# Starting the feed-forward part with the half-token products of two weight pairs, and making their weight sums later

## Chip, core and metric

The kernel runs on one core of one Trainium2 chip. The metric is the device time in microseconds (us), as the median of several executions. One execution was also taken with the hardware profiler; it stands beside the others below. Engines are named as the profile names them: PE (TensorE), PEld (its weight loads), DVE (VectorE), ACT (ScalarE), POOL (GpSimd) and SP (SyncE, which here only issues DMAs). "Lnnn" is a line of the kernel's source.

## The reference

Two layers of a transformer-like block run over 512 tokens of width 1024, all in float32. The change touches the second half of each layer: the norm, the input product of the feed-forward part and what follows.

```python
D_MODEL = 1024
SEQ = 512
DEPTH = 2
FFN_HIDDEN = 2816
...
        x = x + merged @ w_out[i]
        hn = rmsnorm(x, norm2_g[i])
        gate, up = jnp.split(hn @ w_ffn_in[i], 2, axis=-1)
        x = x + (jax.nn.silu(gate) * up) @ w_ffn_out[i]
```

Ahead of these lines stand a combined input projection, a pool mixer, a differential attention and a gated merge, which the change leaves as they are.

## The kernel before

**Precision.** Every float32 operand is cut into a high and a low part of type float32r, `hi` and `lo`, and a product is three matmuls: hi by hi, hi by lo, lo by hi (`product` L243, `pair_product` L253). The usual cut (`split` L177) is a cast on ACT (L179) and a subtraction on DVE (L180). A second form (`parts` L207 with a piece number) relieves DVE: ACT casts the high part (L214), copies it negated into the low part (L215), and POOL issues a DMA that adds the weights from memory on top of it (L216).

**Seven products instead of eight.** The feed-forward input works on pairs of hidden tiles. A pair has 256 gate columns and 256 up columns, and each of its four weight pieces is 512 rows by 256 columns (128x1024 in memory, 512 KB): A11 and A12 are the gate's first and second half of rows, A21 and A22 the up's. The activations are cut the same way into halves of rows and halves of tokens, B11 and B21 for tokens 0 to 255 and B12 and B22 for tokens 256 to 511. A scheme of the Strassen kind makes the four output blocks with seven products of 24 matmuls each (128x256). The class `Ffn` numbers them: 1 is A11 by B11, 2 is A12 by B21, 4 is A22 by T4, and 3, 5, 6, 7 multiply the weight sums S4, S1, S2, S3 (made on DVE, L672 to L678) with B22 and the activation sums T1, T2, T3. Products 1 and 2 need tokens 0 to 255 alone; all others need all 512 tokens. `first` runs product 1, `second` product 2, `rest` the other five in the order 6, 5, 7, 3, 4 (with product 2 between 5 and 7 where it was not done yet), and `swiglu` makes the hidden tile.

**Where the activations come from.** `project_out` (L605) adds the output projection to the residual `res` (L599) token tile by token tile (four tiles of 128). After each tile `normed` (L294) is issued: a square with a sum on ACT (L298), a small operation on DVE (L276), a power on POOL (L277), and two multiplications on DVE into `xs` (L302). `normed` puts the transposition of `xs` on PE (L267, eight 128x128 matmuls) into a list of later work, which is due when a given amount of matmul work has been issued, or when `need` (L285) asks for it. `Quarters.put` (L337) follows each transposition: for tiles 0 and 1 it makes B11 and B21, for tiles 2 and 3 it makes T1 to T4 and B22 out of the transposed values and those of tile 0 or 1 (tiles `xd`; parts `xqh`, `xql`, `xrh`, `xrl`, `xth`, `xtl`; L357 to L367).

**The order around the change.** After `project_out` the first pair (f0 = 0) loads its four pieces, makes all its sets and sums, runs products 1 and 2, waits by `need` for tiles 2 and 3, and runs `rest`. Then the second pair (f0 = 2) begins, with product 2 within `rest`, and so on for eleven pairs in three rounds, with the feed-forward output product after each round. `weight_plan` (L47) lists the pieces in the order in which SP loads them.

**Buffers.** Raw pieces and one sum per pair (`ws`) share seven buffers (`RAWS`), the cut sets six pairs of high and low buffers (`SPLITS`). PSUM has three `mm` tiles, two `sc` tiles (the accumulator `self.a` of products 1 and 2) and two `tr` tiles (the transpositions, and product 4). A scheduler places each engine's instructions when the program is built; at run time each engine takes its instructions strictly in that order.

## Time and profile before

| quantity | value |
|---|---|
| median of 3 runs | 1466.33 us (1463.86 to 1468.88) |
| the profiled execution's own time | 1463.79 us |
| its span, first to last instruction | 1461.9 us |
| mean granted TensorE clock | 0.995 |
| DVE busy | 978.4 us (67%) |
| ACT busy | 698.8 us (48%) |
| POOL busy | 120.6 us (8%) |
| DMA, mean over the span | 118 GB/s |

The span is what the profile's pages count from; the execution's own time is 1.9 us longer. Two stretches per execution concern the change, one for each layer: from the first matmul of product 1 (378.88 us in layer 0, 1102.80 us in layer 1) to the first matmul of the third pair (432.72 and 1156.51 us). Busy times in the profile count an instruction from its start to its modelled end, so that neighbours overlap; the distance from one start to the next is what a row of work costs.

### The profile page before, as it was taken

The page shows a single profiled execution, that of the slowest core. Times are in us where ns is not written, and L with a number is a line of the kernel's source. Part 1 is how long each engine was busy: PE and PEld are TensorE (multiplying, and loading weights), DVE is VectorE, ACT ScalarE, POOL GpSimd, SP SyncE. Part 2 cuts the span into 40 slices and gives each one's busy share as a digit, 9 for nine tenths or more (in the row PEclk, how much of TensorE's full clock was granted, in tenths as well). Part 3 has the DMA queues.
Part 4 walks back from the last instruction along what each step waited for, and adds up shares of the span by engine and source line. Part 5 has one row for each costly group of instructions (what it writes and reads, how often), then busy time and mean ns, then how long its engine had stood idle before and what let it go on. Part 6 is the DMA issues. An engine that isn't in the chain of part 4 may idle for free.

```text
span 1461.9 us, 21648 instructions
## 1 busy us (share of the span) xinstructions
PE 1437.6 (98%) x8390; PEld 1267.7 (87%) x8390; DVE 978.4 (67%) x1816; ACT 698.8 (48%) x1323; POOL 120.6 (8%) x153
## 2 busy tenths in 40 slices
PE   8999999999799999999999999999997999999999
PEld 6888888888699989989888888888887998999897
DVE  7767666666788548736576686666758885487472
ACT  6544353453666346516355443435446663464350
POOL 1010000000101001001010001000001110010000
PEclk9999999999999999999999999999999999999999
DMA  7321231223358447817422132222323774586261
GB/s 278 108 73 62 90 116 58 87 88 99 87 146 191 139 126 179 216 43 207 140 86 81 58 116 80 72 80 68 127 59 101 176 197 114 135 185 176 66 166 58
DMA packets 49784, 173.02 MB, mean 118 GB/s; under 512 B 5649, under 2 KB 6545, under 8 KB 49682
## 3 DMA queue, kind: packets, MB, share of 16 engines
q1 hardware_dynamic: 38882, 134.41, 28.0%
q0 software_dynamic: 9504, 34.61, 13.3%
q10 hardware_dynamic: 1296, 2.62, 0.6%
q8 instruction: 66, 1.08, 0.3%
q14 instruction: 36, 0.29, 0.1%
HBM read 169.52 MB, written 2.10 MB: 117 GB/s over the span
## 4 chain that ended last, share of the span: by engine, by line
PE 95%; DVE 3%; ACT 1%; issue 1%; POOL 0%; DMA 0%; POOLq 0%; DVEq 0%
PE mm L248 19%; PE mm L250 19%; PE mm L249 19%; PE mm L262 6%; PE mm L263 6%; PE mm L260 6%; PE sc L260 3%; PE sc L262 3%; PE sc L263 3%; PE tr L267 3%; PE tr L263 1%; PE tr L262 1%; PE tr L260 1%; DVE wlo L180 1%; PE sc L250 1%; DVE xs L302 1%
## 5 line engine op out<-in xcount | busy, mean ns | idle before, releaser
L179 ACT CAST whi<-raw 128x1024 fp32r<-128x1024 f32 x222 | 233.2, 1052 | 197.3 <-issue 118.7
L180 DVE TENSOR_TENSOR wlo<-raw,whi 128x1024 fp32r<-128x1024 f32 x222 | 270.0, 1220 | 83.9 <-ACT whi L179 79.1
L248 PE MATMUL mm<-whi,xh 128*128 128x512 f32 x512 | 206.1, 402 | 0.1
L250 PE MATMUL mm<-whi,xl 128*128 128x512 f32 x512 | 200.6, 392 | 0.0
L249 PE MATMUL mm<-wlo,xh 128*128 128x512 f32 x512 | 200.5, 392 | 0.1
L599 DVE TENSOR_TENSOR res<-mm,res 128x512 f32<-128x512 f32 (+1 forms) x97 | 66.0, 683 | 118.1 <-PE mm L250 118.0
L250 PE MATMUL mm<-whi,fl 128*128 128x512 f32 (+1 forms) x358 | 138.5, 387 | 0.0
L248 PE MATMUL mm<-whi,fh 128*128 128x512 f32 (+1 forms) x358 | 138.3, 387 | 0.0
L249 PE MATMUL mm<-wlo,fh 128*128 128x512 f32 (+1 forms) x358 | 138.2, 387 | 0.0
L277 POOL TENSOR_TENSOR r<-r,mhalf 128x1 f32<-128x1 f32 (+1 forms) x80 | 62.0, 774 | 671.8 <-DVE r L276 567.4
L250 PEld LDWEIGHTS mm<-whi,xl 128*128 128x128 f32 x512 | 96.3, 188 | 21.1 <-DVE xl L180 0.2
L248 PEld LDWEIGHTS mm<-whi,xh 128*128 128x128 f32 x512 | 96.6, 189 | 18.5 <-ACT xh L179 0.6
L249 PEld LDWEIGHTS mm<-wlo,xh 128*128 128x128 f32 x512 | 96.7, 189 | 17.9 <-DVE wlo L180 0.5
L216 POOL DMA_DIRECT2D wlo<-in_wts x66 | 57.9, 877 | 619.1 <-ACT wlo L215 322.3
L260 PE MATMUL sc<-xqh,whi 128*128 128x256 f32 x352 | 101.9, 289 | 0.7 <-ACT whi L214 0.7
L248 PE MATMUL mm<-xh,whi 128*128 128x512 f32 x256 | 102.0, 398 | 0.0
L260 PE MATMUL mm<-xrh,whi 128*128 128x256 f32 x352 | 99.8, 284 | 1.9 <-ACT xrh L179 1.9
L262 PE MATMUL sc<-xql,whi 128*128 128x256 f32 x352 | 101.1, 287 | 0.0
L263 PE MATMUL sc<-xqh,wlo 128*128 128x256 f32 x352 | 101.0, 287 | 0.0
L262 PE MATMUL mm<-xrl,whi 128*128 128x256 f32 x352 | 99.8, 284 | 0.9 <-DVE xrl L180 0.9
L260 PE MATMUL mm<-xqh,whi 128*128 128x256 f32 x352 | 99.8, 284 | 0.3
L250 PE MATMUL mm<-xh,wlo 128*128 128x512 f32 x256 | 99.9, 390 | 0.0
(161 smaller groups left out, 3463.5 us busy)
## 6 DMA issues: line engine op xcount, KB each, us to landing
raw<-in_wts SPq DMA_DIRECT2D x244, 512.0 KB, 4.3
wlo<-in_wts POOLq DMA_DIRECT2D x66, 512.0 KB, 7.5
pwr<-in_pool_w ACTq DMA_DIRECT2D x8, 256.0 KB, 2.6
out<-res SPq DMA_DIRECT2D x7, 256.0 KB, 2.0
res<-in_x SPq DMA_DIRECT2D x3, 512.0 KB, 8.2
g<-in_gains SPq DMA_DIRECT2D x6, 256.0 KB, 3.1
res<-in_x ACTq DMA_DIRECT2D x1, 512.0 KB, 3.7
lv<-in_rows SPq DMA_DIRECT2D x2, 256.0 KB, 5.7
```

Of the source, the lines that this page charges most:

```text
L179: ins = nc.scalar.copy(hi, src)
L180: nc.vector.tensor_sub(lo, src, hi.bitcast(F32))
L216: nc.gpsimd.dma_start(lo.rearrange("p a b -> p (a b)"), wts[piece_no], accum_op=ALU.add)
L248: nc.tensor.matmul(acc, lhsT=ah, rhs=bh, start=i == 0, stop=False)
L249: nc.tensor.matmul(acc, lhsT=ah, rhs=bl, start=False, stop=False)
L250: nc.tensor.matmul(acc, lhsT=al, rhs=bh, start=False, stop=i == n - 1)
L260: nc.tensor.matmul(acc[:, i, :], lhsT=ah, rhs=bh, start=start and not i and not k, stop=False, skip_group_check=True)
L262: nc.tensor.matmul(acc[:, i, :], lhsT=ah, rhs=bl, start=False, stop=False, skip_group_check=True)
L263: nc.tensor.matmul(acc[:, i, :], lhsT=al, rhs=bh, start=False, stop=i == 1 and k == 3, skip_group_check=True)
L267: nc.tensor.transpose(dst, src, ident)
L277: nc.gpsimd.tensor_tensor(r, r, mhalf[:, :width], op=ALU.pow)
L599: nc.vector.tensor_add(res[t][:, cs], here, res[t][:, cs])
```

## The change

Each layer's feed-forward part begins otherwise; its pairs from the third on are written as before.

1. The plan lists A11 of the first two pairs, then A12 of both, and then A21 and A22 of each of the two pairs.
2. The two `Ffn` objects are made within the last `project_out`, ahead of its token tiles. There A11 and A12 of both pairs are loaded and cut: A11 in the form with POOL's DMA, A12 in the usual form, by ACT and DVE.
3. After `need` for tiles 0 and 1, product 1 runs for both pairs, and then product 2 for both. After `need` for tiles 2 and 3 follow, pair by pair, `sums` (the loads of A21 and A22, the weight sums and the other sets) and `rest`.
4. In `sums` of the first two pairs the set of A22 is made after those of S2 and S1 and ahead of those of S3 and S4. For the other pairs it is made last, as before.
5. In `put` the temporaries T1, T2 and a copy of B22 live in buffers named `us` and `up` instead of `qn`.

```diff
-        def ffn_in(f):
-            gate, up = span((P * f, 256)), span((FF + P * f, 256))
-            for k, cols in ((0, gate), (0, up), (4, up), (4, gate)):
-                plan.append(("w_ffn_in", layer, k, 4, cols))
+        def ffn_in(f, parts):
+            cols = span((P * f, 256)), span((FF + P * f, 256))
+            for k, up in parts:
+                plan.append(("w_ffn_in", layer, k, 4, cols[up]))
...
+        for part in ((0, 0), (4, 0)):
+            for f in (0, 2):
+                ffn_in(f, (part,))
...
-            t1, t2, t3, t4 = temp("qn", 3), temp("qn", 3), temp("ta", 2), temp("ta", 2)
+            t1, t2, t3, t4 = temp("us", 2), temp("us", 2), temp("ta", 2), temp("ta", 2)
...
+            def gate(self, k, piece_no=None):
+                self.sets[1 + k] = parts(self.r12 if k else self.r11, piece_no)
+
+            def sums(self, a12=False):
+
                 _, r21 = loaded()
                 n22, r22 = loaded()
...
+                if a12:
+                    self.gate_raw(1)
                 s1 = sb.tile([P, 4, VD], F32, name="ws", tag="raw", bufs=RAWS)
+                if a12:
+                    self.gate(0, self.n11)
                 nc.vector.tensor_add(s1, r21, r22)
+                nc.vector.tensor_sub(r21, self.r11, r21)
+                nc.vector.tensor_sub(self.r11, s1, self.r11)
+                self.sets[6] = parts(self.r11)
+                self.sets[5] = parts(s1)
+                if a12:
+                    self.gate(1, self.n12)
+                else:
+                    self.sets[4] = parts(r22, n22)
+                nc.vector.tensor_sub(self.r12, self.r12, self.r11)
+                self.sets[7] = parts(r21)
+                self.sets[3] = parts(self.r12)
+                if a12:
+                    self.sets[4] = parts(r22, n22)
...
         def project_out(heads, last):
...
             if last:
                 quarters.append(Quarters())
                 g = gain_row(2 * layer + 1)
+                early.extend(Ffn(f0) for f0 in (0, 2))
+                for f in early:
+                    f.gate_raw(0)
+                for f in early:
+                    f.gate_raw(1)
+                for f in early:
+                    f.gate(0, f.n11)
+                for f in early:
+                    f.gate(1)
...
+        def ffn_start():
+            need(*((f"h{layer}", t) for t in range(2)))
+            for x in early:
                 x.first()
+            for x in early:
                 x.second()
+            need(*((f"h{layer}", t) for t in range(2, 4)))
+            for x in early:
+                x.sums()
                 x.rest()
```

Three places show how the built program moves, all in layer 0 (layer 1 reads the same with other buffer numbers). Source lines of the changed kernel are numbered 3 higher than before up to L602, and otherwise behind it.

**First place: DVE, from the residual of token tile 3 on.** `res3` is that residual, `xs` its normed rows, `r` their factor, `xd_3719` and `xd_3699` the first steps of `put` for tile 2 (out of the transposed `tr`), `wlo` low parts of weight sets. Before:

```order
L599 TENSOR_TENSOR res3_92<-mm_3605,res3_92 128x512
L180 TENSOR_TENSOR wlo_3682<-raw_3659,whi_3681 128x1024
L599 TENSOR_TENSOR res3_92<-mm_3637,res3_92 128x512
L180 TENSOR_TENSOR wlo_3686<-ws_3667,whi_3685 128x1024
L180 TENSOR_TENSOR wlo_3691<-raw_3661,whi_3690 128x1024
L276 TENSOR_SCALAR r_3654<-ss_3652 128x1
L180 TENSOR_TENSOR wlo_3695<-raw_3665,whi_3694 128x1024
L302 SCALAR_TENSOR_TENSOR xs_3651<-res3_92,r_3654,g_3475 128x512
L302 SCALAR_TENSOR_TENSOR xs_3651<-res3_92,r_3654,g_3476 128x512
L357 TENSOR_TENSOR xd_3719<-tr_3709,xw_3568 128x512
L672 TENSOR_TENSOR ws_3975<-raw_3969,raw_3971 128x1024
L358 TENSOR_TENSOR xd_3720<-tr_3714,xd_3719 128x512
```

After, where `raw_3483` and `raw_3485` hold A12 of the two pairs and `raw_3479` holds S2 of the first:

```order
L602 TENSOR_TENSOR res3_92<-mm_3631,res3_92 128x512
L183 TENSOR_TENSOR wlo_3498<-raw_3483,whi_3497 128x1024
L183 TENSOR_TENSOR wlo_3502<-raw_3485,whi_3501 128x1024
L183 TENSOR_TENSOR xql_3470<-xw_3645,xqh_3469 128x4x128
L183 TENSOR_TENSOR xql_3470<-xw_3649,xqh_3469 128x4x128
L602 TENSOR_TENSOR res3_92<-mm_3663,res3_92 128x512
L360 TENSOR_TENSOR xd_3699<-tr_3689,xw_3594 128x512
L183 TENSOR_TENSOR wlo_3856<-raw_3479,whi_3855 128x1024
L279 TENSOR_SCALAR r_3680<-ss_3678 128x1
L361 TENSOR_TENSOR xd_3700<-tr_3694,xd_3699 128x512
L305 SCALAR_TENSOR_TENSOR xs_3677<-res3_92,r_3680,g_3475 128x512
L305 SCALAR_TENSOR_TENSOR xs_3677<-res3_92,r_3680,g_3476 128x512
```

Of the first pair's four low parts of sums only S2's is left here, and the two low parts of A12 have come in; the steps for tile 2 no longer stand behind those of tile 3's norm, and the second pair's sum (`ws_3975`) has gone from between them.

**Second place: PE and ACT, the set of A22 of the first pair.** On PE, `mm_3817` and `mm_3880` are the accumulator of products 5 and 3, `tr_3932` and `tr_3995` that of product 4, whose low part is `wlo_3699` before and `wlo_3864` after. PE before:

```order
L263 MATMUL mm_3817<-xqh_3469,wlo_3695 128x256
L260 MATMUL mm_3817<-xqh_3469,whi_3694 128x256
L262 MATMUL mm_3817<-xql_3470,whi_3694 128x256
L263 MATMUL mm_3817<-xqh_3469,wlo_3695 128x256
L260 MATMUL tr_3932<-xth_3473,whi_3698 128x256
L262 MATMUL tr_3932<-xtl_3474,whi_3698 128x256
L263 MATMUL tr_3932<-xth_3473,wlo_3699 128x256
L260 MATMUL tr_3932<-xth_3473,whi_3698 128x256
L262 MATMUL tr_3932<-xtl_3474,whi_3698 128x256
```

PE after:

```order
L265 MATMUL mm_3880<-xql_3470,whi_3859 128x256
L266 MATMUL mm_3880<-xqh_3469,wlo_3860 128x256
L263 MATMUL tr_3995<-xth_3473,whi_3863 128x256
L265 MATMUL tr_3995<-xtl_3474,whi_3863 128x256
L266 MATMUL tr_3995<-xth_3473,wlo_3864 128x256
L263 MATMUL tr_3995<-xth_3473,whi_3863 128x256
L265 MATMUL tr_3995<-xtl_3474,whi_3863 128x256
L266 MATMUL tr_3995<-xth_3473,wlo_3864 128x256
L263 MATMUL mm_3880<-xqh_3469,whi_3873 128x256
L265 MATMUL mm_3880<-xql_3470,whi_3873 128x256
L263 MATMUL tr_3995<-xth_3473,whi_3863 128x256
L265 MATMUL tr_3995<-xtl_3474,whi_3863 128x256
```

ACT before (`raw_3663` holds A22; the square of tile 3's norm stands ahead of it):

```order
L298 ACTIVATE xs_3651,ss_3652<-res3_92 128x1024
L214 CAST whi_3698<-raw_3663 128x1024
L215 ACTIVATE wlo_3699<-raw_3663 128x1024
L179 CAST xqh_3469<-xd_3719 128x4x128
L179 CAST xrh_3471<-xd_3720 128x4x128
```

ACT after (`raw_3849` holds A22; `xd_3783` belongs to tile 3):

```order
L182 CAST xrh_3471<-xd_3783 128x4x128
L365 COPY xd_3792<-tr_3777 128x512
L218 ACTIVATE wlo_3864<-raw_3849 128x1024
L182 CAST xqh_3469<-xd_3792 128x4x128
L182 CAST xrh_3471<-xd_3784 128x4x128
```

Before, product 4 begins when product 3 is through; now its first three groups of matmuls stand directly behind product 5, ahead of all of product 7 and nearly all of product 3. On ACT the negated copy of A22, which lets POOL issue the adding DMA, has moved from ahead of the steps for tile 2 to among those for tile 3.

**Third place: DVE, from the end of the first pair's product 4 on.** `cpwh` is read from product 4's accumulator, `th` and `fl` belong to `swiglu`; `ws_3975` and `ws_4034` are S1 of the second pair. Before:

```order
L180 TENSOR_TENSOR wlo_3989<-ws_3975,whi_3988 128x1024
L715 TENSOR_TENSOR cta_3894<-mm_3816,cqn_3760 128x512
L718 TENSOR_TENSOR cpwl_3920<-cta_3894,cah_3868 128x512
L678 TENSOR_TENSOR raw_3973<-raw_3973,raw_3967 128x1024
L720 TENSOR_TENSOR cal_3922<-mm_3817,cqn_3842 128x512
L180 TENSOR_TENSOR wlo_3999<-raw_3969,whi_3998 128x1024
L642 SCALAR_TENSOR_TENSOR th_3924<-th_3924,cal_3922 128x512
L642 SCALAR_TENSOR_TENSOR th_3959<-th_3959,sc_3705 128x512
L643 SCALAR_TENSOR_TENSOR th_3924<-th_3924,cpwl_3920 128x512
L725 TENSOR_TENSOR cpwh_3957<-tr_3932,cta_3894 128x512
L180 TENSOR_TENSOR fl_3704<-th_3924,fh_3703 128x256 x2
L643 SCALAR_TENSOR_TENSOR th_3959<-th_3959,cpwh_3957 128x512
```

After:

```order
L711 TENSOR_TENSOR cpwh_4020<-tr_3995,cta_3957 128x512
L612 SCALAR_TENSOR_TENSOR th_3987<-th_3987,cal_3985 128x512
L612 SCALAR_TENSOR_TENSOR th_4022<-th_4022,sc_3685 128x512
L613 SCALAR_TENSOR_TENSOR th_3987<-th_3987,cpwl_3983 128x512
L613 SCALAR_TENSOR_TENSOR th_4022<-th_4022,cpwh_4020 128x512
L183 TENSOR_TENSOR fl_3878<-th_3987,fh_3877 128x256 x2
L183 TENSOR_TENSOR fl_3878<-th_4022,fh_3877 128x256 x2
L183 TENSOR_TENSOR wlo_4043<-ws_4034,whi_4042 128x1024
```

The low part of the second pair's S1 stood ahead of the whole `swiglu` of the first pair and now stands behind it.

More of the change, by code (lines that the diff above doesn't have):

```diff
@@ L601, in add_out @@
                     nc.sync.dma_start(out[token(t), cs], res[t][:, cs])
-        quarters = []
-        def project_out(heads, last):
-            w = [wblock(2 * len(heads)) for cb in range(2)]
-            if last:
-                quarters.append(Quarters())
-                g = gain_row(2 * layer + 1)
-            for t in range(NT):
-                for cb in range(2):
-                    add_out([((ms[j][0][:, a, token(t)], ms[j][1][:, a, token(t)]), w[cb][2 * i + a])
-                             for i, j in enumerate(heads) for a in range(2)], t, cb)
-                if last:
-                    normed(f"h{layer}", t, None, None, g, quarters[-1].put)
-        ms, mjs = {}, {}
-        def mix(i):
-            j = ORDER[i]
-            if i == 2:
-                need(*((layer, ORDER[3], "s", t) for t in range(NT)))
-                ms[j] = pair("m", "qk", 4)
-            else:
-                ms[j] = pair("m", "m", 2)
-            merged(j, mjs[j], *ms[j])
-        for i, j in enumerate(ORDER):
-            then = (lambda: project_out(ORDER[i - 2:i - 1], False)) if i >= 2 else None
-            mjs[j] = attention(j, ORDER[i - 1] if i else None, then)
-            if i:
-                mix(i - 1)
-        mix(3)
-        project_out(ORDER[2:], True)
         hidden = {}
@@ L685, in __init__ @@
+                self.to = hidden_pair(self.f0)
                 for i in range(2):
-                    hidden[f0 + i] = self.to[i]
+                    hidden[self.f0 + i] = self.to[i]
             def temp(self, tag, bufs=1):
@@ L691, in p @@
             def p(self, n, acc, start=True):
-                pair_product(acc, *self.pairs[n], start)
+                q = quarters[-1]
+                x = {1: q.b11, 2: q.b21, 3: q.b22, 4: q.t4, 5: q.t1, 6: q.t2, 7: q.t3}[n]
+                pair_product(acc, self.sets[n], x, start)
             def first(self):
@@ L755, in trunk_kernel @@
             for f in range(f0, f1, 2):
-                ffn_in(f)
+                if f >= 4:
+                    ffn_in(f)
+                elif not f:
+                    ffn_start()
                 if r and f == f0:
```

67 lines of the change are left out of this document (41 added, 26 removed).

## The prediction

> **What bounds the kernel now.** The page comes first, then the chain that ended last, then the waits of PE.
>
> ```profile
> span 1461.9 us, 21648 instructions
> PE 1437.6 (98%) x8390; PEld 1267.7 (87%) x8390; DVE 978.4 (67%) x1816; ACT 698.8 (48%) x1323; POOL 120.6 (8%) x153
> PE 95%; DVE 3%; ACT 1%; issue 1%; POOL 0%; DMA 0%; POOLq 0%; DVEq 0%
> PE tr L267 <- ACT xd L362: 13.0, 2, 6.5
> PE mm L260 <- ACT xrh L179: 1.9, 2, 1.0
> PE mm L262 <- DVE xrl L180: 0.9, 2, 0.5
> ```
>
> PE is the bound, and the matmuls stay the same in number and shape, so only its idle or slow time can change. Nearly all of its waits are of one kind and come twice, once per layer, where the feed-forward part begins. The view by stretches sizes that place (columns: stretch, length, busy time of each engine, granted clock, DMA): the first two pairs of each layer, and behind each the third pair alone.
>
> ```profile
> 378.88:432.72 53.84, 45.41 (x353) 44.16 (x352) 45.48 (x59) 34.35 (x47) 6.67 (x7) 0.94 0.60 141
> 432.72:452.88 20.16, 20.16 (x170) 20.16 (x169) 16.51 (x22) 13.53 (x18) 2.60 (x3) 1.00 0.79 182
> 1102.80:1156.51 53.71, 45.28 (x354) 44.03 (x352) 45.48 (x59) 34.32 (x47) 6.65 (x7) 0.94 0.59 141
> 384.00:388.00 4.00, 0.00 (x0) 0.00 (x0) 3.63 (x5) 1.32 (x2) 1.22 (x2) 0.88 0.91 259
> 392.00:394.00 2.00, 2.00 (x12) 2.00 (x12) 1.55 (x3) 0.62 (x1) 0.00 (x0) 0.54 0.11 23
> ```
>
> A pair without waits takes 20.16 us, or 168 matmuls at 0.12. Two pairs and 16 transpositions (eight take 0.79, from 379.24 to 380.03 in the rows below) need 2 x 20.16 + 1.6 = 41.9 us. The first two pairs take 53.84 and 53.71. So **11.9 us per layer, 23.7 in all,** is the most that the change can win. The rows of PE show what the 11.9 is.
>
> ```profile
> 379.24 1.03 PE L267 MATMUL tr<-ident,xs 128*128 128x128 f32 x8
> 380.03 0.36 PE L260 MATMUL sc<-xqh,whi 128*128 128x256 f32 x1
> 389.31 0.69 PE L267 MATMUL tr<-ident,xs 128*128 128x128 f32 x2 [6.52 <-ACT xd L362]
> 397.19 0.39 PE L260 MATMUL mm<-xrh,whi 128*128 128x256 f32 x1 [0.97 <-ACT xrh L179]
> 398.55 0.38 PE L262 MATMUL mm<-xrl,whi 128*128 128x256 f32 x1 [0.44 <-DVE xrl L180]
> ```
>
> 6.5 us are the wait of tile 3's transposition for a `tr` buffer, which ends when tile 2 has been read out. After it the clock is half: 0.88 over 384 to 388 and 0.54 over 392 to 394 put the half clock from 387.0 to 393.8. PE works in 389.3 to 393.8 of that, so 4.5 us of half speed lose 2.3. The other 3.1 lie around 395 to 398.6, where product 6 waits for T2 of tile 3.
>
> **The change part by part.** What sets these waits is DVE, nearly full there, which makes weight sums between the steps for x:
>
> ```profile
> 375.51 1.41 DVE L302 SCALAR_TENSOR_TENSOR xs<-res,r,g 128x512 f32<-128x512 f32 x2 [0.73 <-POOL r L277]
> 376.84 1.29 DVE L180 TENSOR_TENSOR xql<-xw,xqh 128x512 fp32r<-128x512 f32 x2
> 378.04 0.68 DVE L599 TENSOR_TENSOR res<-mm,res 128x512 f32<-128x512 f32 x1
> 386.30 1.22 DVE L672 TENSOR_TENSOR ws<-raw 128x1024 f32<-128x1024 f32 x1
> 387.43 0.68 DVE L358 TENSOR_TENSOR xd<-tr,xd 128x512 f32<-128x512 f32 x1
> 395.76 0.69 DVE L358 TENSOR_TENSOR xd<-tr,xd 128x512 f32<-128x512 f32 x1
> ```
>
> From start to start a 512-wide step costs 0.60 (376.84 to 378.04 for two), a 1024-wide one 1.14 (386.30 to 387.43), the pair of `xs` 1.33 (375.51 to 376.84).
>
> *When x is ready.* Up to 376.84 nothing on the path is new. In the new order DVE then has, up to the second `xd` of tile 3 (395.76 before): three 1024-wide low parts, fourteen 512-wide steps (six in the first place shown, then two low parts, `xd`, low part, `xd`, low part for tile 2, `xd` for tile 3, `xt` low part), the `xs` pair and the small `r`: 3.42 + 8.4 + 1.33 + 0.06 = 13.2. It starts at 390.1, 5.6 us earlier. With itself, two more 512-wide steps and one 1024-wide, T2's low part of tile 3 is there at 393.1.
>
> *PE up to there.* Its first triple at 378.88 is followed by tile 2's transpositions; the next matmul needs B11's low part of tile 1, which now stands behind the two A12 low parts: 376.84 + 0.60 + 2.28 + 0.60 = 380.3, a new wait of **0.5**. Then 95 matmuls of products 1 and 2 and eight transpositions, 11.4 + 0.8, end at 392.5, and six matmuls of products 6 and 5 can go before T2 is needed. So the 6.5, the 2.3 and the 3.1 vanish: twice as many half-token products cover the steps for x. Tile 3's transposition finds its `tr` buffer free.
>
> One duration on this path is open, the power on POOL between `r` and `xs` of tile 3:
>
> ```profile
> 374.92 0.55 POOL L277 TENSOR_TENSOR r<-r,mhalf 128x1 f32<-128x1 f32 x1 [5.78 <-DVE r L276]
> 382.93 1.40 POOL L277 TENSOR_TENSOR r<-r,mhalf 128x1 f32<-128x1 f32 x1 [7.46 <-DVE r L276]
> 385.00 0.89 POOL L216 DMA_DIRECT2D wlo<-in_wts  x1 [0.67 <-ACT wlo L215]
> ```
>
> It took 0.55 beside an idle DVE and 1.40 beside a 1024-wide subtraction. Now it runs beside `xd`, 0.60 long; I take 0.55 and keep 1.40 as the end.
>
> *Product 4 of the first pair.* This is what is late next. Its low part comes by POOL's DMA. ACT's negated copy stands three places behind that `xd` of tile 3:
>
> ```profile
> 388.15 0.62 ACT L179 CAST xrh<-xd 128x512 fp32r<-128x512 f32 x1 [1.11 <-DVE xd L358]
> 389.15 0.59 ACT L698 COPY cqn<-sc 128x512 f32<-128x512 f32 x1
> 383.65 1.05 ACT L215 ACTIVATE wlo<-raw 128x1024 fp32r<-128x1024 f32 x1
> ...
> DMA to landing us min/median/max: 5.4/7.6/9.0
> wlo<-in_wts POOLq DMA_DIRECT2D x1, 512.0 KB, 8.2
> ```
>
> For tile 2 the third ACT place came at 389.15, 1.72 after its `xd` (387.43). So the copy starts at 390.1 + 1.7 = 391.8. POOL issues 1.35 after a copy's start (383.65 to 385.00): 393.2. The adding DMAs of 380 to 460 us landed 5.4 to 9.0 after issue. The one issued at 385.00 took 8.2, with two loads beside it; here the loads of the second pair's A21 and A22 go out in the same microsecond, because the first pair's buffers come free then. I take 8.2: landed at 401.4 (ends 398.6 and 402.2). PE reaches the first matmul that needs it after 50 matmuls, 392.5 + 6.0 = 398.5, since product 4's first groups now stand ahead of products 7 and 3, which wait behind it in PE's strict order. **New wait 2.9** (0.1 to 3.7).
>
> [...]
>
> *S1 of the second pair.* After 401.4 the first pair has 70 matmuls left, to 409.8. Only then can `cpwh` be read; behind it on DVE stand four `th`, four `fl` and then S1's low part (third place).
>
> ```profile
> 414.03 0.68 DVE L725 TENSOR_TENSOR cpwh<-tr,cta 128x512 f32<-128x512 f32 x1
> 414.63 0.75 DVE L180 TENSOR_TENSOR fl<-th,fh 128x256 fp32r<-128x256 f32 x2
> 415.30 0.69 DVE L643 SCALAR_TENSOR_TENSOR th<-th,cpwh 128x512 f32<-128x512 f32 x1
> ```
>
> That is 0.60 + 4 x 0.60 + 2 x 0.67 + 1.14 = 5.5, to 415.3. PE has 30 matmuls until it needs it (product 6, and two each of products 5, 4 and the third pair's 1 that go ahead): 3.6, to 413.4. **New wait 1.9**; with 0.1 to 0.2 of latency 2.1, ends 1.4 and 2.8. Before, S1 stood ahead of the whole `swiglu`.
>
> *The sets behind it.* The second pair's A22 and the third pair's A11 are copied on ACT only behind that `swiglu`'s casts, at about 413.6 and 414.5, so POOL issues both DMAs at about 415 and 416 beside three loads. Needed: 70 and 92 matmuls after 415.4, at 423.8 and 426.4. At 7.7 the first lands at 422.7, in time. The second stands behind it in POOL's queue:
>
> ```profile
> q0 software_dynamic: 9504, 34.61, 13.3%
> ```
>
> 13.3% of the span for 66 of them is 2.95 us each, so it lands between 423.6 and 426.6, up to 428 with 9.0. The fourth and fifth pair meet the same crowd. I take **1.5** for all of these, ends 0 and 4.
>
> *Parts at nothing.* Two negated copies and two adding DMAs per layer become two low parts on DVE; they are counted in the 13.2. The loads of the second pair's A21 and A22, now late for want of raw buffers, land at about 399; DVE is busy with x and the first pair's sets until 400. The temporaries in `us` and `up` use buffers that lie idle then.
>
> **Sum.** Per layer 0.5 + 2.9 + 2.1 + 1.5 = 7.0 of new waits for 11.9 of old ones: 4.9 won, 9.8 for both. The profiled execution took 1463.8, so 1454.0; the median of the runs, 1466.3, is 2.5 above it, and the forecast goes by the median: **1456.5 us.** The ends of the new waits are 2.0 (0.5, 0.1, 1.4, 0) and 11.0 (0.5, 3.7, 2.8, 4).
>
> **Rivals.**
> - *All covered.* A22 lands in 5.4 and the crowd does no harm: new waits 2.0, 9.9 won per layer, 1466.3 - 19.8 = 1446.5. For it: that landing was seen once, with no load beside it. Against: here loads are beside it. Chance 0.18.
> - *The adding DMAs become the bound.* PE is 5 us further on, the ACT copies are not, and each adding DMA up to the fifth pair is late: new waits 11.0, won 0.9 per layer, 1464.5. For it: POOL's DMAs are issued in twos at 1 us, and landings up to 9.0. Against: every stall gives the next DMA time. Chance 0.22.
> - *Slower: the clock drops twice.* If a wait at product 4 reaches some 4.5 us (landing 9.0 and one ACT place later), it may be long enough for the half clock, whose stretch before was 6.8 us, 3.4 of work. With that in both pairs, new waits are 0.5 + 4.5 + 3.4 + 2.1 + 4.5 + 3.4 = 18.4, lost 6.5 per layer: 1479. One pair alone only gives the win back. The point from which it decides lies between 1 and 6.5 us. Chance 0.12. [...]
> - That the order doesn't change is excluded by the rows shown.
>
> **How the numbers follow.** The forecast, 1451 to 1462, has 0.48. A measurement of this kernel tells about 0.3%, 4.4 us, from no change. Below 1461.9 lie the forecast and the first rival: faster 0.66. Within 0.3%: the second rival, 0.22. Slower: the third, 0.12. The range is 1447 to 1467: from all covered to the second rival's upper side, leaving out the clock's case.
>
> **What would show it.** Right: no `tr` wait for `xd` of 6.5, a clock of 1.00 throughout, T2's part before 394, and instead a PE wait for a POOL DMA at product 4 of about 3 us and one for DVE's `wlo` of about 2. Wrong: no such waits (first rival), waits for `wlo` in the third to fifth pair of more than 2 us (second), a PEclk of 0.50 behind product 4 (third).

## The result, and the profile after

The changed kernel takes 1457.16 us (median of 6 executions, 1456.47 to 1458.65), the kernel before 1465.07 (6 executions beside it, 1463.14 to 1468.88): a ratio of 0.995, 95% interval 0.994 to 0.996. So it is faster by half a per cent. The profiled execution took 1456.47, against 1463.79 before. First the lines of the page that answer to those of before:

```profile
span 1454.4 us, 21625 instructions
PE 1435.9 (99%) x8390; PEld 1266.9 (87%) x8390; DVE 980.6 (67%) x1820; ACT 692.8 (48%) x1319; POOL 115.3 (8%) x149
q0 software_dynamic: 8928, 32.51, 12.6%
```

PE does the same 8390 instructions and is busy 99% of a span that is 7.5 us shorter. Its waits (engine, line, what for: us in total, times, longest) have changed their names:

```profile
PE tr L266 <- DMA wlo<-in_wts: 4.7, 2, 2.5
PE mm L266 <- DVE wlo L183: 4.7, 2, 2.3
...
PE sc L265 <- DVE xql L183: 0.8, 2, 0.4
...
PE sc L266 <- DMA wlo<-in_wts: 0.3, 1, 0.3
```

The waits for `xd` (13.0) and for the parts of T2 are gone. In their place product 4 of the first pair (`tr`) waits for A22's adding DMA, product 5 of the second pair (`mm`) for S1's low part, each once per layer. The next view is that by stretches (stretch, length, busy time of PE, PEld, DVE, ACT, POOL, granted clock, DMA share, GB/s): the stage in both layers, then three pieces of layer 0.

```profile
379.28:431.98 52.70, 47.51 (x377) 46.64 (x376) 48.84 (x67) 32.24 (x47) 4.07 (x5) 0.97 0.46 122
1099.31:1151.86 52.55, 47.27 (x378) 46.60 (x377) 48.34 (x66) 32.25 (x47) 4.06 (x5) 0.97 0.45 122
400.17:403.59 3.42, 2.04 (x17) 2.04 (x18) 3.35 (x4) 0.00 (x0) 0.00 (x0) 1.00 0.98 337
413.83:417.24 3.41, 1.07 (x9) 1.02 (x9) 3.41 (x7) 2.52 (x5) 1.43 (x2) 1.00 0.24 53
417.24:420.65 3.41, 3.41 (x18) 3.41 (x17) 3.38 (x5) 0.08 (x1) 0.33 (x1) 0.50 1.02 189
```

The stage now holds the third pair's product 1 too, 24 matmuls of 0.12. Without it, the stage takes 52.70 - 2.88 = 49.8 us where it took 53.84, and 49.7 where it took 53.71: 4.0 won in each layer. Of the 11.9 us above the bare work, 7.9 are left. And the clock is not 1.00: it is half for one piece of 3.41 us behind the S1 wait, 18 matmuls in place of some 30. In the piece ahead of it PE works 1.07 us (31%); in the piece around the wait at product 4 it works 2.04 (60%), and the clock stays full behind that. The rows of the timeline (start, duration, engine, line, operation, output and inputs, and in brackets PE's wait) show the steps of the forecast:

```profile
392.38 1.06 ACT L218 ACTIVATE wlo<-raw 128x1024 fp32r<-128x1024 f32 x1
392.99 0.69 DVE L183 TENSOR_TENSOR xrl<-xd,xrh 128x512 fp32r<-128x512 f32 x1
393.74 0.90 POOL L219 DMA_DIRECT2D wlo<-in_wts  x1 [9.25 <-DVE xrl L183]
401.55 0.39 PE L266 MATMUL tr<-xth,wlo 128*128 128x256 f32 x1 [2.19 <-DMA wlo<-in_wts]
414.94 1.22 DVE L183 TENSOR_TENSOR wlo<-ws,whi 128x1024 fp32r<-128x1024 f32 x1
415.76 1.81 POOL L219 DMA_DIRECT2D wlo<-in_wts  x2 [21.13 <-ACT wlo L218]
416.22 0.39 PE L266 MATMUL mm<-xqh,wlo 128*128 128x256 f32 x1 [2.34 <-DVE wlo L183]
429.26 0.38 PE L266 MATMUL sc<-xqh,wlo 128*128 128x256 f32 x1 [0.25 <-DMA wlo<-in_wts]
```

T2's low part of tile 3 (`xrl`) is done at 393.7, in time. A22's copy starts at 392.38, POOL issues at 393.74, PE goes on at 401.55. S1's low part starts at 414.94. The two adding DMAs of 415.76 (the second pair's A22, the third pair's A11) are the crowd of the forecast; it costs 0.25 in layer 0 and nothing in layer 1. Yet they land late, 9.5 and 12.5 us after issue, where the forecast took 7.7 and at most 9.0:

```profile
DMA to landing us min/median/max: 9.5/11.0/12.5
```

PE hardly waits for them because it comes late itself, held up by the S1 wait and the half clock.

### The profile page after: what moved, and what is told of

It is laid out like the page before. It is cut to its first block, busy times and chain, and to the rows that moved or that the text cites. A ratio compares the mean times of both kernels' runs of the same rounds, so it can differ in the third digit from the quotient of the medians.

```text
span 1454.4 us, 21625 instructions
## 1 busy us (share of the span) xinstructions
PE 1435.9 (99%) x8390; PEld 1266.9 (87%) x8390; DVE 980.6 (67%) x1820; ACT 692.8 (48%) x1319; POOL 115.3 (8%) x149
## 4 chain that ended last, share of the span: by engine, by line
PE 92%; issue 3%; DVE 2%; DMA 2%; ACT 1%; POOL 0%; POOLq 0%; DVEq 0%
PE mm L251 19%; PE mm L253 19%; PE mm L252 19%; PE mm L266 5%; PE mm L263 5%; PE mm L265 5%; PE sc L265 3%; PE sc L266 3%; PE sc L263 3%; PE tr L270 3%; DMA wlo<-in_wts 1%; PE tr L266 1%; PE tr L263 1%; PE tr L265 1%; DVE wlo L183 1%
## 5 line engine op out<-in xcount | busy, mean ns | idle before, releaser
L182 ACT CAST whi<-raw 128x1024 fp32r<-128x1024 f32 x226 | 237.4, 1052 | 210.8 <-issue 120.1
L183 DVE TENSOR_TENSOR wlo<-raw,whi 128x1024 fp32r<-128x1024 f32 x226 | 274.6, 1221 | 81.7 <-ACT whi L182 77.5
L602 DVE TENSOR_TENSOR res<-mm,res 128x512 f32<-128x512 f32 (+1 forms) x97 | 66.1, 684 | 118.7 <-PE mm L253 118.6
L266 PE MATMUL mm<-xqh,wlo 128*128 128x256 f32 x352 | 101.2, 288 | 4.7 <-DVE wlo L183 4.7
L219 POOL DMA_DIRECT2D wlo<-in_wts x62 | 54.3, 876 | 614.9 <-ACT wlo L218 328.2
L265 PE MATMUL mm<-xql,whi 128*128 128x256 f32 x352 | 100.9, 287 | 0.0
```

The source lines that it names most:

```text
L182: ins = nc.scalar.copy(hi, src)
L183: nc.vector.tensor_sub(lo, src, hi.bitcast(F32))
L219: nc.gpsimd.dma_start(lo.rearrange("p a b -> p (a b)"), wts[piece_no], accum_op=ALU.add)
L265: nc.tensor.matmul(acc[:, i, :], lhsT=ah, rhs=bl, start=False, stop=False, skip_group_check=True)
L266: nc.tensor.matmul(acc[:, i, :], lhsT=al, rhs=bh, start=False, stop=i == 1 and k == 3, skip_group_check=True)
L602: nc.vector.tensor_add(res[t][:, cs], here, res[t][:, cs])
```

## The experiments

Each was timed beside the kernel before on the same chip. The changed kernel is the base of all; diffs are cut to their core. e1 to e4, e5 to e8, e9 and e10, e11 and e12 were timed in four groups, in which the kernel before had medians of 1464.48, 1465.18, 1465.42 and 1465.50; so times of different groups compare to about 1 us.

| run | what | us, median (lowest to highest) | ratio to before, 95% interval |
|---|---|---|---|
| the change | | 1457.16 (1456.47 to 1458.65) | 0.995 (0.994 to 0.996) |
| e1 | first pair's A22 by DVE | 1453.58 (1453.03 to 1454.21) | 0.9924 (0.9911 to 0.9937) |
| e2 | second pair's S1 ahead of swiglu | 1468.33 (1464.25 to 1470.27) | 1.002 (1.001 to 1.003) |
| e3 | PE filled at S1 | 1456.02 (1455.43 to 1457.30) | 0.9941 (0.993 to 0.9953) |
| e4 | one pair early | 1465.23 (1463.32 to 1466.65) | 1.0002 (0.9993 to 1.001) |
| e5 | sums ahead of x | 1454.77 (1453.69 to 1456.52) | 0.993 (0.9917 to 0.9942) |
| e6 | four sets by DVE | 1451.19 (1450.35 to 1451.46) | 0.9903 (0.989 to 0.9917) |
| e7 | e6, PE filled at S1 | 1450.62 (1450.19 to 1451.23) | 0.9901 (0.9886 to 0.9916) |
| e8 | A22 made last | 1464.06 (1460.39 to 1467.98) | 0.9994 (0.9984 to 1.0004) |
| e9 | e5, PE filled at product 6 | 1450.09 (1450.06 to 1450.17) | 0.99 (0.9884 to 0.9917) |
| e10 | parts put together | 1451.53 (1449.51 to 1452.27) | 0.9908 (0.9893 to 0.9923) |
| e11 | the change, PE filled at both waits | 1449.10 (1448.95 to 1449.35) | 0.9886 (0.9869 to 0.9902) |
| e12 | e10, PE filled at product 6 | 1449.64 (1449.34 to 1449.79) | 0.9888 (0.9874 to 0.9903) |

### What the parts of the change are worth (e4, e5, e8)

**One pair early (e4).**

```diff
-        for part in ((0, 0), (4, 0)):
-            for f in (0, 2):
+        for part in ((0, 0), (4, 0)):
+            for f in (0,):
...
-                early.extend(Ffn(f0) for f0 in (0, 2))
+                early.extend(Ffn(f0) for f0 in (0,))
```

> Half of the change alone: only the first pair's half-token products come early, the second pair is made as before; the first pair's sums stay behind the steps for x. Theory 1, what hides the steps for x are the 96 half-token matmuls of two pairs: with 48 (5.8 us) PE comes to product 6 of the first pair at about 386.5, T2's low part of tile 3 is ready at about 390 to 391 (two 1024-wide low parts less on DVE), so waits of 4 to 5 us come back in each layer, with the half clock, and with the set that product 2 of the second pair needs late behind them; 1461 to 1466. Theory 2, it is the place of the sums behind the steps for x that wins, and the second pair only adds the S1 and DMA waits: the time is that of the change or less, 1453 to 1458.

The time is that of the kernel before, as theory 1 said, but by another wait than it named. The rows of PE, one for each layer:

```profile
397.39 0.55 PE L266 MATMUL sc<-xqh,wlo 128*128 128x256 f32 x1 [7.61 <-DMA wlo<-in_wts]
1120.95 0.55 PE L266 MATMUL sc<-xqh,wlo 128*128 128x256 f32 x1 [6.38 <-DMA wlo<-in_wts]
```

After the first pair's products 1 and 2, and ahead of its product 6, PE's order has the second pair's product 1, which waits for A11's adding DMA (the last one issued ahead of it goes out at 390.74). Two shorter waits stand ahead of it in each layer, 1.80 for a copy on ACT (`cqn`) and 0.68 for `xd`. So PE stands still at half-token work whose weights aren't ready, and not at product 6. How long T2 alone would have kept it waiting can't be read here: e4 shows that one pair wins nothing in this order, not what it could win in another.

**Sums ahead of x (e5).** `early[0].sums()` stands ahead of `first()` again.

```diff
+            early[0].sums()
             for x in early:
                 x.first()
...
             for x in early:
-                x.sums()
+                if x.f0:
+                    x.sums()
                 x.rest()
```

> The other half of the change alone: both pairs' half-token products come early, but the first pair's sums are made ahead of them again, among the steps for x. On DVE five 1024-wide steps then stand ahead of T2's low part of tile 3 where one stands with the change, so that part comes 4 x 1.14 = 4.6 us later, at about 398.3; PE is through the half-token products and six matmuls more at about 394. Theory 1, the place of the sums only trades one wait for others: 4.2 us and a half clock at product 6 come back, but A22's adding DMA and the second pair's S1 are then early, and their 2.4 + 2.4 + 1.7 go; the time is within 3 us of the change, 1455 to 1460. Theory 2, sums behind x are what wins: the 4.2 and the half clock come on top of waits that stay, 1457.2 + 2 x 5.9 = 1469.

Theory 1, and a little better than it said: the waits for the adding DMA and for S1 are gone, and one of 3.36 at product 6 is back, with the half clock. Timeline of PE, then the stretches around it:

```profile
396.49 0.39 PE L263 MATMUL mm<-xrh,whi 128*128 128x256 f32 x1 [3.36 <-ACT xrh L182]
...
1115.07 0.58 PE L263 MATMUL mm<-xrh,whi 128*128 128x256 f32 x1 [3.36 <-ACT xrh L182]
```

```profile
393.55:396.96 3.41, 0.47 (x4) 0.47 (x5) 3.41 (x6) 2.21 (x5) 0.00 (x0) 1.00 0.36 137
396.96:400.37 3.41, 3.21 (x16) 2.92 (x15) 3.41 (x6) 1.65 (x3) 0.00 (x0) 0.50 0.00 0
1110.35:1113.76 3.41, 1.36 (x11) 1.06 (x10) 3.41 (x7) 1.81 (x3) 0.00 (x0) 1.00 0.88 317
1113.76:1117.17 3.41, 2.10 (x9) 1.98 (x10) 3.41 (x6) 1.78 (x4) 0.00 (x0) 0.50 0.01 2
1117.17:1120.58 3.41, 3.41 (x18) 3.41 (x18) 3.41 (x6) 1.24 (x2) 0.00 (x0) 0.50 0.00 0
```

So moving the sums behind x isn't what wins; it trades one wait of 3.4 for two of 2.2 to 2.5. The same wait of 3.36 brought one half piece in layer 0 and two in layer 1.

**A22 made last (e8).**

```diff
-                else:
-                    self.sets[4] = parts(r22, n22)
...
-                if a12:
-                    self.sets[4] = parts(r22, n22)
+                self.sets[4] = parts(r22, n22)
```

> One part of the change undone: A22's set of the first two pairs is made last again, behind S3 and S4. ACT then copies A22 of the first pair behind S4's cast (ends at about 398.4), at about 399.5 to 400.5 instead of 392.4, so its adding DMA lands at about 408.5. Products 7 and 3 go ahead of product 4. Theory 1, A22 in third place is worth its wait: S3 and S4's low parts make PE wait about 1.2 at 399, then A22 about 2.4 at 406, against 2.4 before; and the second pair's A22, copied last behind the swiglu, is late too, by 2 to 5 us: 1460 to 1468. Theory 2, the place does not matter since the adding DMA is covered by products 7 and 3: 1457 or less.

Theory 1: the whole win is lost. The first pair's A22, copied at 398.68 in place of 392.38, keeps PE waiting 2.22 and 2.88 at 408 and 1132, and the second pair's A22 is later still:

```profile
427.67 0.36 PE L266 MATMUL tr<-xth,wlo 128*128 128x256 f32 x1 [3.77 <-DMA wlo<-in_wts]
...
1153.65 0.36 PE L266 MATMUL tr<-xth,wlo 128*128 128x256 f32 x1 [3.54 <-ACT wlo L218]
```

(In layer 1 the view names an ACT copy that ended at that moment; the last two adding DMAs ahead of this wait had gone out from 1145.42 on.)

The change of the temporaries' tags can't be undone alone: the copies of both pairs' product 1 hold two of the three `qn` buffers, and the steps for x would need three. It was not tried.

### What the new waits cost (e1, e2, e3)

**A22 of the first pair by DVE (e1).** `BY_DVE` lists the sets, by pair and product, that DVE cuts.

```diff
+BY_DVE = {0: (4,)}
...
-                    self.sets[4] = parts(r22, n22)
+                    self.sets[4] = parts(r22, None if 4 in BY_DVE.get(self.f0, ()) else n22)
```

> Only A22's low part of the first pair is changed: DVE cuts it (1.14 us from start to start) instead of a negated copy on ACT and an adding DMA, so product 4 of the first pair no longer waits for a DMA (2.4 to 2.5 us in each layer with the change). Theory 1, the remaining waits add up: this wait goes, the later ones stay as they are, and the time falls by 2 x 2.4 = 4.9, from 1457.2 to 1452. Theory 2, the waits stand behind one another on DVE and on the adding DMAs: PE arrives 2.4 earlier at S1 of the second pair and at the third pair's A11, DVE has 1.14 more ahead of S1, the adding DMA of A11 is no earlier; so these two waits take up most of the 2.4, and the time is 1456 to 1458.

The time, 3.6 us below the change, lies between the two theories. The wait at product 4 is gone and the S1 wait stays as it was, so DVE had the 1.14 to spare; but the third pair's A11 is late. The scheduler's order moves a little with the set, on PE too (product 4's matmuls). The rows of PE, and the stretches around the S1 wait:

```profile
413.95 0.39 PE L268 MATMUL mm<-xqh,wlo 128*128 128x256 f32 x1 [2.35 <-DVE wlo L185]
427.64 0.35 PE L268 MATMUL sc<-xqh,wlo 128*128 128x256 f32 x1 [1.86 <-DMA wlo<-in_wts]
...
1132.45 0.39 PE L268 MATMUL mm<-xqh,wlo 128*128 128x256 f32 x1 [2.35 <-DVE wlo L185]
1146.02 0.35 PE L268 MATMUL sc<-xqh,wlo 128*128 128x256 f32 x1 [0.55 <-DMA wlo<-in_wts]
```

```profile
409.75:413.17 3.42, 1.84 (x16) 1.64 (x14) 3.42 (x8) 3.24 (x7) 0.00 (x0) 1.00 0.00 0
413.17:416.58 3.41, 2.63 (x22) 2.64 (x22) 3.41 (x4) 1.44 (x2) 0.90 (x1) 1.00 0.76 208
1129.97:1133.38 3.41, 1.06 (x9) 0.93 (x8) 3.41 (x6) 1.66 (x4) 0.89 (x1) 1.00 0.22 56
1133.38:1136.79 3.41, 3.41 (x18) 3.41 (x17) 3.41 (x5) 2.00 (x2) 0.00 (x0) 0.50 0.95 244
```

This is the most telling pair of rows in the study. One and the same wait of 2.35 is followed by half clock in layer 1 and not in layer 0. And where PE lost 1.7 to the half clock, A11's DMA kept it waiting 0.55, where not, 1.86: the half clock and the crowd of adding DMAs cover each other. Of the 3.4 us between the two profiled executions (1456.47 and 1453.03), 1.7 are the one half piece less. The two waits that went had cost 5.3 from start to start (2.5 and 2.8), so the greater part of them came back: 2.4 at A11, the rest in delays too short for the view of waits.

**S1 ahead of the swiglu (e2).** `sums` is cut in two behind S1's set; `between` runs ahead of the second `swiglu` of the first pair.

```diff
-            for x in early:
-                x.sums()
-                x.rest()
+            early[0].sums()
+            early[0].rest(between=early[1].sums_ahead)
+            early[1].sums_behind(False)
+            early[1].rest()
```

> Only the order is changed: the first five sums and the sets S2 and S1 of the second pair come ahead of the second swiglu of the first pair, not behind it. With the change S1's low part starts at 414.94, behind cpwh, four th and four fl, though its high part lies ready from 406.4. Theory 1, the place behind the swiglu makes the S1 wait (2.4 us per layer) and this wait makes the half clock (3.41 us, 1.7 lost per layer): both go, 2 x 4.1 = 8.2, so 1449, and the clock is 1.00 in that place. Theory 2, the S1 wait only covers what is late behind it: the second pair's A22 is copied on ACT later or at the same time as now, its adding DMA lands 7 to 9 us after that, and PE waits 2 to 5 us for it at product 4 of the second pair, with or without half clock; then 1455 to 1465.

Theory 2, and worse: 11 us slower than the change. The S1 wait is gone, and PE waits for adding DMAs instead, at product 4 of the second pair and at the third pair's A11:

```profile
PE tr L266 <- DMA wlo<-in_wts: 9.4, 4, 2.5
PE sc L266 <- DMA wlo<-in_wts: 4.4, 2, 2.4
```

Two of the four in the first line, 2.22 and 2.21, are the first pair's, as with the change; new are 2.55 and 2.44 at the second pair, and the 2.39 and 1.99 of the second line. POOL issues the second pair's A22 at 414.32 and the third pair's A11 at 419.62; with the change both go from 415.76 on. PE, no longer held at S1, comes to product 4 earlier, and A11's DMA goes out some 3 us later, since its copy on ACT stands behind `cah`, which waits for PE (1.99 us, until 417.72). The profile shows half clock in four pieces. So the S1 wait had been hiding these DMAs.

**PE filled at S1 (e3).** The order of all else is unchanged.

```diff
+                if self.f0 == 2:
+                    for i in range(16):
+                        nc.tensor.transpose(oy[:, 0, :P], self.sets[6][1][:, 0, :P].bitcast(F32), ident)
                 self.p(5, c)
```

> Added work alone: 16 transpositions of 128x128 in each layer, into a PSUM tile that nothing reads, on PE between product 6 of the second pair and the matmul that waits for S1 (some 1.7 us of the 2.4 us wait). Theory 1, the half clock behind this wait comes from PE's idle time in it: the clock stays 1.00, 1.7 us per layer are won though PE does more, 1453.8. Theory 2, the half clock has another cause (the load of the DMA or of the other engines at that place) or the wait is not what it seems: the half clock of 3.41 us stays in both layers and the time stays at 1457 (up to 1460 if the transpositions delay anything).

More work on PE, and no slower: 1.1 us below the change. Behind the S1 wait the clock is 1.00 in both layers, as theory 1 says:

```profile
417.47 0.39 PE L266 MATMUL mm<-xqh,wlo 128*128 128x256 f32 x1 [0.61 <-DVE wlo L183]
```

Without the transpositions PE would have been idle here from about 415.1 to 417.47, most of the piece from 415.35 to 418.77 (an estimate from the last matmul ahead of them, at 414.60, and 0.12 for each of the two behind it). But only part of the 3.4 came out. In this profile the wait at product 4 of layer 0, 2.38 long, is the one that brought half clock (401.70 to 405.11), and adding DMAs keep PE waiting 0.59 and 0.78 in layer 0 and 0.59 in layer 1 behind it.

### Half clock, measured by itself (e9), and the sum of the parts (e6, e7, e10, e11, e12)

**Sums ahead, PE filled at product 6 (e9).** In e5 nothing waits behind product 6, so that a gain there can't come back as another wait.

```diff
+                if not self.f0:
+                    for i in range(24):
+                        nc.tensor.transpose(oy[:, 0, :P], self.sets[2][1][:, 0, :P].bitcast(F32), ident)
                 self.p(6, b)
```

> As the experiment with the first pair's sums ahead of x (median 1454.8), with 24 transpositions of 128x128 added on PE in each layer ahead of product 6, into a PSUM tile that nothing reads. In that experiment's profile product 6 waits 3.36 us for T2 of tile 3 in each layer, and half clock follows: 3.41 us in layer 0 and 6.83 in layer 1, where PE works some 3.4 and 5.5 us, so that 1.7 + 2.8 = 4.5 us are lost. Theory 1, PE's idle share within a stretch sets the half clock: the transpositions (2.6 us) keep the stretch busy, no half clock, 1450.3. Theory 2, the half clock comes from what the other engines and DMAs do there: it stays, 1454 to 1456.

4.7 us won over e5 where 4.5 were forecast, by 48 transpositions whose results nobody reads.

```profile
396.79 0.39 PE L263 MATMUL mm<-xrh,whi 128*128 128x256 f32 x1 [0.69 <-ACT xrh L182]
```

Product 6 waits 0.7 and starts 16.25 us behind B11's first low part, as in e5 (380.54 to 396.79, and 380.25 to 396.49), so DVE and ACT bring its input no earlier. A few of their instructions and of PE's change places ahead of it and behind it; but no wait of PE above 0.2 us stands behind it in either kernel, so a gain in the order there can't be what won. The clock is 1.00 where e5 has 0.50: with the transpositions in PE's wait the half clock is gone, and theory 2 falls, as it does in e3, where every engine keeps its order. The four executions lie within 0.11 us.

**Four sets by DVE (e6), and PE filled at S1 (e7).** e6 has `BY_DVE = {0: (4,), 4: (1, 2, 4)}`; e7 adds the 16 transpositions of e3.

> On top of the first experiment (A22 of the first pair cut by DVE), the third pair's A11, A12 and A22 are cut by DVE too, 3 x 1.14 = 3.4 us more of DVE per layer and three adding DMAs less. Theory 1, what is left behind the S1 wait are late adding DMAs (1.86 and 0.55 us at the third pair's A11 in the first experiment): they go, 1453.6 - 2.4 = 1451. Theory 2, DVE is the bound from the second to the fourth pair: its 3.4 us come out as waits for low parts of the third or fourth pair, 1454 to 1460.

> As the kernel before it in this call (four sets of the first and third pair cut by DVE), with 16 transpositions added in the wait for S1 of the second pair, into a PSUM tile that nothing reads. If the half clock comes when PE does little within one stretch of 3.41 us, and the wait of 2.35 at S1 meets such a stretch in one execution and not in another (in the first experiment's profile in layer 1 but not in layer 0), then the transpositions take it away: 1449 to 1450.5, and the times of the executions lie within 1 us of one another. If the half clock is of another kind, the time is that of the kernel without them, 1451, or above.

e6 came out as theory 1 said. The S1 wait stays; the profiled execution shows it in both layers, without half clock in either:

```profile
414.21 0.39 PE L268 MATMUL mm<-xqh,wlo 128*128 128x256 f32 x1 [2.34 <-DVE wlo L185]
446.65 0.36 PE L268 MATMUL sc<-xqh,wlo 128*128 128x256 f32 x1 [0.46 <-DMA wlo<-in_wts]
...
1131.33 0.39 PE L268 MATMUL mm<-xqh,wlo 128*128 128x256 f32 x1 [2.35 <-DVE wlo L185]
```

So e7 had little to win in such executions: 0.6 us between the medians, within their scatter, and a mean clock of 1.000 in all four (0.999 in three of e6's, about what one half piece in 1450 us makes). Its range of 1449 to 1450.5 was missed by 0.1, and the executions lie within 1.04 us.

**The parts put together (e10, e12).** S2, S1, A22 and S3 of the first pair ahead of x, S4 behind, `BY_DVE = {2: (4,), 4: (4,), 6: (1,)}`; e12 adds 13 transpositions ahead of product 6.

```diff
+            early[0].sums_ahead()
             for x in early:
                 x.first()
...
+            early[0].sums_behind(False)
+            early[0].rest()
+            early[1].sums()
+            early[1].rest()
```

> The parts put together: two pairs of half-token products early, as in the change; the first pair's sums and the sets S2, S1, A22 and S3 ahead of the steps for x, S4's subtraction and set behind them (two 1024-wide steps less ahead of T2 than in the experiment with all sums ahead); A22 of the second and third pair and A11 of the fourth cut by DVE (1.14 each) instead of an adding DMA. Theory 1, the waits are those of DVE's order alone: 3.36 at product 6 shrinks by 1.3 to 2.3 to between 1.1 and 2.1, too little for a half clock in most executions, and nothing is late behind it: 1454.8 - 2 x 1.5 - 4.5 = 1447.5 (1446 to 1449). Theory 2, what PE gains comes out at the next adding DMA (third to fifth pair): 1451 or more.

> As the mixed version (median 1451.5, executions 1449.5 to 1452.3, at a mean clock of 1.0 in the fastest and 0.999 in the others), with 13 transpositions of 128x128 on PE ahead of product 6 of the first pair, where it waits 1.76 us, into a PSUM tile that nothing reads. Theory 1, the executions above 1449.5 have a half clock in one layer, set by that wait: with it filled all come to 1449.5. Theory 2, the half clock there belongs to another wait (0.9 to 1.1 at the third pair): 1451 to 1452 as before.

e10 missed its forecast by 4 us; its theory 2, with 1451 or more, came true. Product 6 waits 1.76, as forecast, but the third pair's product 1 is kept waiting as well, once by a late cast and once by an adding DMA:

```profile
425.56 0.36 PE L268 MATMUL sc<-xqh,wlo 128*128 128x256 f32 x1 [0.88 <-ACT whi L184]
...
1142.45 0.35 PE L268 MATMUL sc<-xqh,wlo 128*128 128x256 f32 x1 [1.06 <-DMA wlo<-in_wts]
```

e12 came out as its theory 1 said: all four executions have a clock of 1.000 and come close to the fastest of e10, the only one there with that clock. That fits a half clock set by the wait of 1.76 in the other three; no profile of one of those shows it. The waits at the third pair (1.16 and 0.84) are still there.

**The change, PE filled at both waits (e11).** The 16 transpositions of e3, and as many ahead of product 4 of the first pair.

```diff
+                if not self.f0:
+                    for i in range(16):
+                        nc.tensor.transpose(oy[:, 1, :P], self.sets[5][1][:, 0, :P].bitcast(F32), ident)
                 self.p(4, d)
```

> The change with 32 transpositions of 128x128 added on PE in each layer, into a PSUM tile that nothing reads: 16 ahead of product 4 of the first pair, 16 ahead of the matmul that waits for S1 of the second pair. With them the matmuls of product 4 stand together behind products 7 and 3 on PE. Theory 1, the change still pays for half clock in two to four stretches of an execution (1.7 us each; its executions show a mean clock of 0.996 to 0.998): without PE idle at either place it pays for none, 1457.2 - 3 x 1.7 = 1452 and the waits that are left are below 1 us, with executions within 1 us of one another and a clock of 1.00. Theory 2, the fill at S1 alone gave 1456.0 because the time that PE gains comes back at the adding DMAs behind: the same again, 1455 to 1457.

8 us below the change, with 64 transpositions more: the fastest kernel of the study. Of PE's waits only those at the start of the kernel, B11's low part and 0.2 us elsewhere are left:

```profile
PE sc L404 <- DMA row<-in_gains: 2.3, 1, 2.3
PE tr L270 <- DVE xs L305: 1.4, 1, 1.4
PE sc L265 <- DVE xql L183: 0.8, 2, 0.4
PE tr L270 <- DVE xl L183: 0.2, 1, 0.2
```

The result is beyond theory 1 by 3 us, and not by the clock alone. With the transpositions the order moves too: product 4 stands as a whole behind products 7 and 3, so PE asks for A22's DMA at 406 and not at 399; S1's low part stands ahead of the swiglu (at 407.81); and POOL issues the second pair's A22 at 410.07, 4.3 us before e2 does. Between the two profiled executions (1456.47 and 1448.95) the clock accounts for 3.4 of the 7.5 us, two half pieces at 1.7. The rest is in the main the order's: waits that it doesn't have, less the time of the transpositions. In the medians the clock's share can be larger, since four of the change's six executions have a lower clock than the profiled one (0.996 and 0.997, against 0.998).

## Why the prediction came out right, step by step

The forecast was 1456.5 us (1454.0 for the profiled execution); measured were 1457.2 and 1456.5. The time came closer than the win did: 9.8 us were forecast, and 7.9 lie between the medians, 7.3 between the profiled executions. The forecast stood on a median of 1466.3 from three executions, 1.3 above the 1465.07 of six, and this made up for most of the difference. That part is luck.

The terms follow, per layer. The forecast's go from start to start, so the measured ones are the idle time of the rows and 0.27 more for each wait: the last matmul ahead of it counts as busy for 0.28 where the next could start after 0.12, and the first two behind it start 0.23 apart.

| term | forecast | layer 0 | layer 1 |
|---|---|---|---|
| B11's low part of tile 1 | 0.5 | 0.7 | 0.7 |
| product 4 waits for A22's DMA | 2.9 | 2.5 | 2.8 |
| second pair's S1 | 2.1 | 2.6 | 2.6 |
| the sets behind it | 1.5 | 0.5 | 0 |
| half clock | 0 | 1.7 | 1.7 |
| sum | 7.0 | 8.0 | 7.8 |

The stretches above, 7.9 and 7.8 over the bare work, agree with the sums. So the new waits cost 0.8 to 1.0 more per layer than forecast, and 4.0 were won in place of 4.9.

- **The old waits go** (6.5 + 2.3 + 3.1): right. T2's part was forecast for 393.1 and done at 393.7, and tile 3's transposition found its buffer.
- **Product 4.** Right to 0.7 us at each step: copy at 392.38 (forecast 391.8), issue at 393.74 (393.2), PE there at 399.2 (398.5) and on at 401.55 (401.4). e1 shows that only part of this wait is real cost: without it the time falls by 3.6, and between the profiled executions half of the gain is a half piece less. Of the 5.3 that the waits had cost, the greater part came back, mostly at A11's DMA.
- **S1.** The mechanism is right, the wait half a microsecond longer: PE came at 413.7 (forecast 413.4), the low part 0.8 later than forecast. The 0.1 to 0.2 for latency was the author's estimate; from the end of the low part (414.94 + 1.22) to PE's start at 416.22 it is 0.06.
- **"A clock of 1.00 throughout"** is the step that failed. The forecast put the point from which a wait costs half clock between 1 and 6.5 us, looked for it behind product 4 only, and gave the likeliest case none. That a wait of 2.9 leaves the clock full was the author's estimate, and no run shows it. What the runs show is that the waits at product 4, 2.19 and 2.53, were followed by full clock, and that one of 2.38 at the same place in e3 was followed by half. After the change the clock dropped behind the S1 wait of 2.34, in both layers, and took 3.41 us at half speed, 1.7 lost each.
- **The sets behind it** were forecast 1.5 and measured 0.5 and 0, though the landings in layer 0 (9.5 and 12.5) were worse than the worst that the forecast took, 9.0. This miss and the last one cover each other in part: PE, slowed by the half clock, comes to the third pair's A11 at 428.8 and not at 426.4. In e1, in the layer without half clock, this wait is 1.86; with it, 0.55.
- **"What sets these waits is DVE, which makes weight sums between the steps for x"** was half the truth. e5 puts the first pair's sums back between those steps and is no slower than the change. What the win hangs on, in the order as built, is that both pairs' half-token products come early (e4: none of it is left without the second pair, though there by a late DMA) and that A22 is made third (e8: none of it is left without that).
- **The rivals.** *All covered*: no, PE waits at both places. *The adding DMAs as the bound*: not in the change, but it is what e2 and e8 turn into, and part of what e3 and e10 miss. *Slower, the clock drops twice*: half clock behind a wait did come, at 2.34 where it assumed 4.5; its price was too high, since one piece of 3.41 at half costs 1.7, not 3.4, and it takes the place of DMA waits.

## What to carry to other kernels

A wait on the bounding engine may be covering a later one: take one wait away at a time and look for what comes late behind it before counting the gain (e1 kept part of it, e2 lost more than it). Where PE waited amid dense work, 3.36 us in e5 and 2.34 after the change, work without a use put into the wait paid, with a clock of 1.00 behind it where it had been 0.50: 4.7 us in e9, where nothing was late behind the wait, but 1.1 in e3, where adding DMAs were. The copy on ACT that starts the first pair's adding DMA began 9.17 us before the product that needed it went on (392.38 to 401.55), so its place on ACT's queue is worth more than its own microsecond (1.06).

## What the runs showed of the hardware

**Half clock came in pieces of 3.413 us on one grid, and the length of the wait alone did not tell where.** In each profile of this study that has half clock in these stages, all its beginnings lie on one grid of 3.413 us: in e2 at 402.06, 422.54, 443.02 and 1129.10, which is 6, 6 and 201 pieces apart; after the change at 417.24 and 1137.46, 211 apart. Laid out on the grid, the pieces of these profiles part by how long PE worked in them at full clock. In the eight profiles that show half clock (before, the change, e1 to e5 and e8) all 17 pieces from 330 us on in which PE worked, at full clock, for 44% or less were followed by half clock, and all with 51% or more by full clock. e6, which shows none, has one piece between, if its grid is taken from where its first record of full clock begins, at 13.40 (before, that moment and the first half clock, 11.55 and 387.02, are 110 pieces apart; after the change, 11.06 and 417.24, 119). The three closest to the border are one of e8, one of e2 and this one of e6:

```profile
1151.73:1155.14 3.41, 1.49 (x12) 1.52 (x13) 0.79 (x1) 1.81 (x3) 0.86 (x1) 1.00 1.05 263
1155.14:1158.55 3.41, 3.41 (x18) 3.41 (x17) 1.02 (x2) 0.00 (x0) 0.00 (x0) 0.50 0.99 192
```

```profile
1146.17:1149.58 3.41, 1.75 (x14) 1.75 (x15) 3.09 (x5) 0.22 (x1) 0.86 (x1) 1.00 0.98 311
1149.58:1152.99 3.41, 3.41 (x31) 3.41 (x30) 0.29 (x1) 0.00 (x0) 0.00 (x0) 1.00 0.95 201
```

```profile
1129.56:1132.97 3.41, 1.64 (x13) 1.64 (x14) 3.41 (x5) 1.40 (x2) 0.89 (x1) 1.00 0.41 129
```

1.49 of 3.41 is 44%, and half clock follows; 1.75 is 51% and 1.64 is 48%, and it doesn't. The wait of 2.35 in e1 fell within one piece in layer 1 (31% busy), and the half piece behind it cost 1.7 us; in layer 0 it fell across two (54 and 77%), and full clock followed both. Waits of 2.21 and 2.22 in e2, each within a piece with 35% of work, were followed by half clock. Full clock came back behind half pieces in which PE worked for 93% or more; one at 62% (e5, from 1113.76) and one at 74% (e8, from 1131.24) were each followed by a second half piece.

**In two executions with the same order the grid fell in different places, and the time went with the clock.** The profiles of the change and of e3 have the same order on every engine, yet from the end of the wait for B11's low part to the half clock it is 36.39 us in one (380.85 to 417.24) and 21.29 in the other (380.41 to 401.70), which differ by 4.42 pieces and not by a whole number. The kernel before spread over 1463.2 to 1468.7 us in 23 executions, at a mean clock from 0.995 down to 0.992, which is 4.4 us of 1466; e9, whose waits from 330 us on are 0.69 at most, over 0.11 us at 1.000. So most of the scatter of the kernel before goes with the clock. That the grid's place is what moves the clock there is likely and not shown, since one execution of each kernel was profiled.
